# A two-block SwiGLU layer on one core: the first block's projections kept in written order, with row writes, loads and sums rearranged

## The chip, the cores and the metric

One core of one Trainium2 chip. The metric is the device time of one execution, in microseconds. Three runs of the kernel before gave 1728.53 (median), 1725.32 and 1729.53. The engines are named as the profile names them: PE is TensorE (PEld its weight loads), DVE is VectorE, ACT is ScalarE, POOL is GpSimd, SP is SyncE, which here only issues transfers.

## The reference, cut to what matters

One decoder layer on 1024 tokens of width 1024, in float32. The first and the last of its three sub-layers are SwiGLU feed-forward blocks (inner width 2816), between them stands a mix of sliding-window attention and a diagonal state-space model (SSM). Shift, scale and gate of each sub-layer come from one conditioning vector c:

```python
mod = silu(c) @ w_ada[l] + b_ada[l]
(sh1, sc1, ga1, sh2, sc2, ga2, sh3, sc3, ga3) = split(mod, 9)
h = rms_norm(x, g_pre_ff1) * (1 + sc1) + sh1
f = (silu(h @ w1_gate) * (h @ w1_up)) @ w1_down
x = x + 0.5 * ga1 * rms_norm(f, g_post_ff1)
...
```

The middle block adds `ga2 * rms_norm(mixed, g_post_mix)`, the last does as the first with sh3, sc3, ga3 and its own weights. The SSM's tables (powers of its eigenvalues, scaled input and output matrices) depend on parameters alone.

## The kernel before, in words

**Precision and products.** Every large operand is split into a high part rounded to fp32r, cast by ACT (L69), and a low part, the remainder, subtracted by DVE (L70). A product is three matmuls, high x high, high x low, low x high (`mm3`, L74 to L76). The gate and up projections and the down projection go by a Strassen-Winograd scheme: seven products of half-size blocks for eight, with sums and differences of blocks made on DVE.

**A feed-forward block.** `GateUp` computes column unit by column unit: an even unit is a gate, the next odd one the matching up projection. The first two units are computed plainly (`first`, then `first_done` with SiLU and product), since the sums of the activations (`s12`, `s34`) are not there yet. The other 20 units, u = 2 to 21, are in `rest`: for each, seven products in the order 1, 5, 6, 2, 7, 3, 4, each of 12 matmuls of 128x512, in all 140 products. `Weights.conv(i + 3)` (L287) first sees to it that the operands up to product i + 2 are converted: it forms a difference of weight blocks where the product wants one (L295 to L302), then the high and the low part, in one of four slots w0 to w3. `step` then issues the matmuls and what follows: product 1, 5 and 6 are copied out by ACT (L424 to L428), the next product of the chain adds to the same bank, DVE adds the others (L420), and then SiLU (even unit) or the product with the SiLU result (odd unit, L412). At the end of a pair of units four sums of result blocks (L383, `sums`) are written to DRAM for the down projection: on DVE in the first block, on POOL in the second. The results live in eight slots h0 to h7 in rotation, so the copy of product 1 of the next pair (c11) goes into a slot that the sums of the pair before still read.

**Beside the first block.** After each product a hook (`hook1`, L1353) runs. From product 4 on it keeps up to five rows of w_ada in flight (POOL issues the loads, 512 KB each) and reduces one of them on DVE against SiLU(c) to a column of `modc` (L141) at products with i % 8 in (0, 2, 3, 5, 6), 56 in all. After the last come `gate_row` and `scale_cols`: a gate column of 128x8 times its gain is written to DRAM as a row of 1024 (L152), to be read back later as a row broadcast to all partitions (`load_row`, L159). Then the twelve parts of the SSM preparation (`prep_steps`, L1036) follow, one at every third product: a long chain of operations on 128x16 tiles (`step_base`, with two exponentials `exp_`), angles and sines (`step_tw`), then products with transposes on PE (L1191) and small matmuls (L1226). They use slots q0 to q7.

**Then** the down projection (`down`, L453): six products over 11 steps each and a last one in pieces; the results of its first product are copied to q4 to q7 (L552). The mix follows, and the second block with no hook and no preparation.

**What sets the order.** The kernel is written for a framework that orders each engine's instructions when the program is built: an instruction is taken when it is ready by the scheduler's own estimate of time, and of those ready the one written earlier goes first. So an instruction whose inputs are there early can float far ahead of its place, and two products can be exchanged. `tc.keep_in_program_order(x)` ties x behind the instruction written just before it on the same engine; `tc.high_priority()` lets a section rank as if written earlier. The order is fixed on the chip.

## Time and profile before

| | |
|---|---|
| median of three runs | 1728.53 us (1725.32 to 1729.53) |
| profiled execution, its own time | 1731.16 us |
| its span, first to last instruction | 1729.2 us |
| mean granted PE clock | 0.982 |
| PE busy | 1661.3 us, 96% |
| DVE busy | 1261.4 us, 73% |
| ACT busy | 799.8 us, 46% |
| POOL busy | 201.5 us, 12% |
| chain that ended last, by engine | PE 81%, DVE 10%, ACT 3%, DMA 3%, issue 3% |

The page gives shares over the whole span, which mixes stages: PE is busy nearly always, so what matters is where it is not, and what ended each of these idle times. That is read from the windows (busy time by stage), the waits (who waited for whom) and the timeline (single instructions). A matmul's printed duration is longer than the time to the next one's start, since they are pipelined; losses are read from start to start.

### The profile page before, as it was taken

Reading aid. Unit: us, or ns where it says so; the run is one execution under the profiler, and the core shown is the slowest. Engines: PE = TensorE matmul, PEld = TensorE weight load, DVE = VectorE, ACT = ScalarE, POOL = GpSimd, SP = SyncE. Lnnn points to the kernel's source line nnn. Section 1 sums busy time; section 2 is a strip of 40 time slices with the busy share of each in tenths; the row PEclk is TensorE's granted clock in tenths of the full one; section 3 lists DMA queues with packets and bytes.
Section 4 is the critical chain, followed back from the end, with each engine's and each line's share of the span. In section 5 each row is a group of like instructions: output and inputs, shape, how many; then the busy total and the mean of one; then the engine's idle time right before and its main releaser. Section 6 shows DMA issues by size and latency. Waiting matters only on the chain.

```text
span 1729.2 us, 22074 instructions
## 1 busy us (share of the span) xinstructions
PE 1661.3 (96%) x7666; PEld 1357.8 (79%) x7666; DVE 1261.4 (73%) x2434; ACT 799.8 (46%) x1613; POOL 201.5 (12%) x198
## 2 busy tenths in 40 slices
PE   5999998999999999899989998999999999999998
PEld 4878777878787888688767886878888888888886
DVE  7988886899979658736479468776666555687586
ACT  4633333334334457746474157643333333354562
POOL 0011110110210000000003044011211111110001
PEclk8999999999999999899999999999999999999999
DMA  9156665633388342610053035222332323394334
GB/s 376 41 213 213 213 215 198 214 124 128 136 290 315 104 126 79 210 37 25 1 159 111 0 110 196 72 85 104 102 130 92 103 93 110 105 394 141 108 104 160
DMA packets 110624, 248.02 MB, mean 143 GB/s; under 512 B 11952, under 2 KB 27584, under 8 KB 110512
## 3 DMA queue, kind: packets, MB, share of 16 engines
q1 hardware_dynamic: 99776, 209.40, 35.5%
q0 software_dynamic: 10160, 36.16, 6.4%
q8 instruction: 60, 0.98, 0.2%
q10 hardware_dynamic: 576, 1.05, 0.2%
q14 instruction: 52, 0.43, 0.1%
HBM read 186.82 MB, written 59.75 MB: 143 GB/s over the span
## 4 chain that ended last, share of the span: by engine, by line
PE 81%; DVE 10%; ACT 3%; DMA 3%; issue 3%; POOL 0%; SPq 0%; DVEq 0%; ACTq 0%; POOLq 0%
PE b L76 25%; PE b L75 25%; PE b L74 25%; DVE a L70 2%; DVE w L70 1%; PE b L700 1%; PE b L788 1%; PE b L790 1%; PE b L789 1%; DMA g_d<-h 1%; PE b L734 1%; DMA t<-g_d 1%; ACT a L69 1%; PE b L172 0%; PE b L879 0%
## 5 line engine op out<-in xcount | busy, mean ns | idle before, releaser
L74 PE MATMUL b<-a,w 128*128 128x512 f32 x1260 | 493.9, 396 | 21.4 <-ACT w L69 10.0
L75 PE MATMUL b<-a,w 128*128 128x512 f32 x1260 | 495.8, 394 | 4.7 <-DVE a L70 4.7
L76 PE MATMUL b<-a,w 128*128 128x512 f32 x1260 | 488.0, 394 | 3.0 <-DVE w L70 3.0
L74 PEld LDWEIGHTS b<-a,w 128*128 128x128 f32 x1260 | 239.9, 191 | 77.3 <-ACT w L69 13.6
L75 PEld LDWEIGHTS b<-a,w 128*128 128x128 f32 x1260 | 239.8, 190 | 55.7 <-DVE a L70 6.2
L76 PEld LDWEIGHTS b<-a,w 128*128 128x128 f32 x1260 | 239.6, 190 | 56.0 <-DVE w L70 6.1
L69 ACT CAST w<-r 128x512 fp32r<-128x512 f32 (+1 forms) x210 | 130.8, 626 | 212.9 <-PE b L76 169.9
L70 DVE TENSOR_TENSOR w<-r,w 128x512 fp32r<-128x512 f32 (+1 forms) x206 | 151.5, 738 | 96.4 <-ACT w L69 96.4
L75 PE MATMUL b<-w,r 128*128 128x512 f32 x528 | 206.1, 391 | 2.1 <-DVE w L70 2.1
L76 PE MATMUL b<-w,r 128*128 128x512 f32 x528 | 205.7, 390 | 0.0
L74 PE MATMUL b<-w,r 128*128 128x512 f32 x528 | 177.6, 389 | 0.7 <-ACT w L69 0.7
L69 ACT CAST r<-a 128x512 fp32r<-128x512 f32 x110 | 68.5, 623 | 148.9 <-PE b L76 76.1
L70 DVE TENSOR_TENSOR r<-a,r 128x512 fp32r<-128x512 f32 x110 | 77.7, 706 | 76.3 <-ACT r L69 76.1
L420 DVE TENSOR_TENSOR h<-h,b 128x512 f32<-128x512 f32 x120 | 82.1, 685 | 56.7 <-PE b L76 50.9
L75 PEld LDWEIGHTS b<-w,r 128*128 128x128 f32 x528 | 99.7, 189 | 23.5 <-DVE w L70 2.8
L70 DVE TENSOR_TENSOR w<-t,w 128x512 fp32r<-128x512 f32 (+1 forms) x114 | 80.7, 709 | 49.1 <-ACT w L69 48.9
L74 PEld LDWEIGHTS b<-w,r 128*128 128x128 f32 x528 | 99.1, 188 | 21.7 <-ACT w L69 1.1
L76 PEld LDWEIGHTS b<-w,r 128*128 128x128 f32 x528 | 99.7, 189 | 20.6
L383 POOL TENSOR_TENSOR h<-h,h 128x512 f32<-128x512 f32 x44 | 72.1, 1650 | 367.4 <-DVE h L412 316.6
L69 ACT CAST w<-t 128x512 fp32r<-128x512 f32 (+1 forms) x114 | 70.3, 617 | 60.4 <-DVE t L298 27.6
L70 DVE TENSOR_TENSOR w<-a,w 128x512 fp32r<-128x512 f32 x110 | 77.4, 704 | 4.1 <-ACT w L69 3.9
L141 DVE CUSTOM_DVE_ANT_0 q<-q,c,cols 128x1024 f32<-128x1024 f32 x56 | 71.6, 1279 | 3.5 <-DMA q<-in_w_ada 3.5
(371 smaller groups left out, 2569.9 us busy)
## 6 DMA issues: line engine op xcount, KB each, us to landing
r<-in_w_gu SPq DMA_DIRECT2D x88, 512.0 KB, 4.1
g_d<-h SPq DMA_DIRECT2D x154, 256.0 KB, 3.1
q<-in_w_ada POOLq DMA_DIRECT2D x56, 512.0 KB, 4.7
a<-g_d SPq DMA_DIRECT2D x110, 256.0 KB, 2.8
a<-in_w_d SPq DMA_DIRECT2D x88, 256.0 KB, 5.4
a<-in_w_ada SPq DMA_DIRECT2D x16, 512.0 KB, 10.2
a<-in_x SPq DMA_DIRECT2D x12, 512.0 KB, 7.2
x_d<-a SPq DMA_DIRECT2D x12, 512.0 KB, 4.1
```

Source lines behind the costliest of these rows:

```text
L69: act.copy(hi, src)
L70: eng.tensor_tensor(lo, src, hi.bitcast(F32), op=SUB)
L74: pe.matmul(psum, wh, xh, start=first, stop=False, skip_group_check=goes_on)
L75: pe.matmul(psum, wh, xl, start=False, stop=False, skip_group_check=goes_on)
L76: pe.matmul(psum, wl, xh, start=False, stop=last, skip_group_check=goes_on)
L141: return dve.tensor_tensor_reduce(w, w, crow, 1.0, b_ada[:, j : j + 1], MUL, ADD, modc[:, j : j + 1])
L383: self.eng.tensor_tensor(d, x, y, op=op)
L420: dve.tensor_tensor(dst, dst, pb, op=ADD)
L700: pe.matmul(pb[kv][:, m % 2, ks], qT[m][rows, t * P : (t + 1) * P], kT[rows, (t + 1 - nk) * P : (t + 1) * P], start=True, stop=True,)
L734: pe.transpose(pt[:, m, :], pr[4 * kv + m][:, b * P : (b + 1) * P], ident)
L788: pe.matmul(pb, hh, wh, start=k == 0, stop=False)
L789: pe.matmul(pb, hh, wl, start=False, stop=False)
```

## The change

- A function `pinned` runs a function and ties each instruction that it writes behind the last one so written on the same engine. `rest` of the first block passes its `conv` and `step` through it, and `hook1` the column step (`ada_step`), so PE, ACT, DVE, POOL and SP take these in written order. The second block passes a plain call.
- `conv` is parted in two: `sum(n)` makes the loads and the difference for operand n, and is now called for the next operand behind the present one's low part.
- The columns are reduced at products with 1 <= i % 14 <= 8 (from product 4 on) instead of i % 8 in (0, 2, 3, 5, 6).
- A gate row is turned on PE (128x8 to 8x128) and copied by ACT to `rows`, and the write to DRAM takes eight rows of 128 numbers.
- The weights of unit 3 are loaded with those of unit 2, and the four sums of the first pair are written with high priority. These two and the parted `conv` hold for both blocks.
- In the preparation, the first operation of each exponential and the square of `are` are tied behind what is written before them on DVE.

```diff
@@ -74,6 +74,23 @@
...
         pe.matmul(psum, wl, xh, start=False, stop=last, skip_group_check=goes_on)
+
+    last_of = {}
+
+    def pinned(f, *args):
+
+        traced = nc.cur_bb.bb.instructions
+        n = len(traced)
+        r = f(*args)
+        for i in list(traced[n:]):
+            prev = last_of.get(i.engine)
+            if prev is not None:
+                tc.add_manual_dep(
+                    i, prev.name, mybir.DependencyInfo(mybir.DependencyClass.NoSync, mybir.DependencyReason.DATA),
+                    reason="pinned",
+                )
+            last_of[i.engine] = i
+        return r

...
@@ -90,6 +107,7 @@
...
     sink = cp.tile([P, NH], F32, name="sink")
+    rows = cp.tile([8, 3, P], F32, name="rows")

...
@@ -149,7 +167,10 @@
...
             dve.tensor_tensor(g, mod(v), gains[:, 2 * n + 1, :], op=MUL)
-        pool.dma_start(row_d[n].rearrange("(k p) -> p k", p=P), g)
+        pt = bank(tr_rot(), [P])
+        pe.transpose(pt[0:8, :], g, ident)
+        act.copy(rows[:, n, :], pt[0:8, :])
+        pool.dma_start(row_d[n].rearrange("(k p) -> k p", p=P), rows[:, n, :])

...
@@ -263,6 +284,7 @@
...
             self.raw, self.state, self.ops, self.n = {}, {}, {}, 0
+            self.src, self.summed = {}, set()
             self.r_rot = Rot(*names("r", 0, 1, 2, 3))
...
@@ -284,30 +306,39 @@
...

+        def sum(self, n):
+
+            if n >= len(self.seq) or n in self.summed:
+                return
+            self.summed.add(n)
+            u, m = self.seq[n]
+            for i in range(2):
+                self.load(u, i)
+            r0, r1, st = self.raw[u, 0], self.raw[u, 1], self.state[u]
+            b11, b12, b21, b22 = r0[:, 0], r0[:, 1], r1[:, 0], r1[:, 1]
+            if m == "5":
+                dve.tensor_tensor(b11, b12, b11, op=SUB)
+            if m == "6":
+                st["t2"] = slot(self.t_rot(), [512])
+                dve.tensor_tensor(st["t2"], b22, b11, op=SUB)
+            if m == "7":
+                dve.tensor_tensor(b12, b22, b12, op=SUB)
+            if m == "4":
+                dve.tensor_tensor(st["t2"], b21, st["t2"], op=SUB)
+            self.src[n] = {"1": b11, "6": st.get("t2"), "2": b21, "5": b11, "7": b12, "3": b22, "4": st.get("t2")}[m]
+
         def conv(self, upto):
...
                 u, m = self.seq[self.n]
-                for i in range(2):
-                    self.load(u, i)
-                r0, r1, st = self.raw[u, 0], self.raw[u, 1], self.state[u]
-                b11, b12, b21, b22 = r0[:, 0], r0[:, 1], r1[:, 0], r1[:, 1]
-                if m == "5":
-                    dve.tensor_tensor(b11, b12, b11, op=SUB)
-                if m == "6":
-                    st["t2"] = slot(self.t_rot(), [512])
-                    dve.tensor_tensor(st["t2"], b22, b11, op=SUB)
-                if m == "7":
-                    dve.tensor_tensor(b12, b22, b12, op=SUB)
-                if m == "4":
-                    dve.tensor_tensor(st["t2"], b21, st["t2"], op=SUB)
-                src = {"1": b11, "6": st.get("t2"), "2": b21, "5": b11, "7": b12, "3": b22, "4": st.get("t2")}[m]
+                self.sum(self.n)
                 op = slot(self.w_rot(), [2, 512], F32R)
-                split(op[:, 0], op[:, 1], src)
+                split(op[:, 0], op[:, 1], self.src.pop(self.n))
                 self.ops[u, m] = op
...
                         self.load(u + 2, i)
+                self.sum(self.n)

...
@@ -368,7 +399,8 @@
...
             if r == 1:
-                self.sums(0, [slot(o_rot(), [512]) for _ in range(4)])
+                with tc.high_priority():
+                    self.sums(0, [slot(o_rot(), [512]) for _ in range(4)])

...
@@ -383,7 +415,7 @@
...

-        def rest(self, hook):
+        def rest(self, hook, pin):
             U = {}
...
@@ -438,8 +470,8 @@
...
             for i, (u, m) in enumerate(wt.seq):
-                wt.conv(i + 3)
-                step(u, m)
+                pin(wt.conv, i + 3)
+                pin(step, u, m)
                 hook(i)
...
@@ -1045,7 +1077,7 @@
...
             y, n, r, q, m = T("ex_y"), T("ex_n"), T("ex_r"), T("ex_q"), T("ex_m")
-            dve.tensor_scalar(y, x, -150.0, 89.0, op0=MAX, op1=MIN)
+            tc.keep_in_program_order(dve.tensor_scalar(y, x, -150.0, 89.0, op0=MAX, op1=MIN))
             dve.tensor_scalar(n, y, 1.4426950408889634, BIG, op0=MUL, op1=ADD)
...
@@ -1134,7 +1166,7 @@
...
             dve.tensor_scalar(nr, pr[:, :, 1], 1.0, None, op0=SUB)
-            dve.tensor_tensor(t1, are, are, op=MUL)
+            tc.keep_in_program_order(dve.tensor_tensor(t1, are, are, op=MUL))
             dve.tensor_tensor(t2, aim, aim, op=MUL)
...
@@ -1337,6 +1369,8 @@
...
             g.wt.load(2, i)
+        for i in range(2):
+            g.wt.load(3, i)
         g.first_done(0)
...
@@ -1350,13 +1384,13 @@
...

-    def hook1(i):
+    def ada_step(i):
         if i >= 4 and (ada_rest or ada_raw):
...
                 ada_raw.append((j, ada_load(j, rest_rot())))
-            if i % 8 in (0, 2, 3, 5, 6):
-                tc.keep_in_program_order(ada_block(*ada_raw.pop(0)))
+            if 1 <= i % 14 <= 8:
+                ada_block(*ada_raw.pop(0))
             if not ada_raw:
...
@@ -1364,6 +1398,10 @@
...
                 prep.extend(prep_steps())
+
+    def hook1(i):
+        if ada_rest or ada_raw:
+            pinned(ada_step, i)
         elif prep and i % 3 == 0:
...
@@ -1373,7 +1411,7 @@
...

-    g1.rest(hook1)
+    g1.rest(hook1, pinned)
     ins, us, late, shares = mix_streams()
...
@@ -1427,7 +1465,7 @@
...
     second_half(g2)
-    g2.rest(lambda i: None)
+    g2.rest(lambda i: None, lambda f, *args: f(*args))
     down(2, a["w2_d"], None, lambda i: None, lambda: None)
...
```

## Rows read from the trace of the kernel before

**Rows 1.** Windows: the 140 products of each block (time, busy us and counts, clock, DMA)

```profile
84.80:495.20 410.40, 396.22 (x1762) 320.35 (x1761) 355.46 (x660) 151.22 (x264) 54.84 (x87) 0.99 0.54 182
1127.50:1512.60 385.10, 383.10 (x1682) 316.56 (x1681) 234.88 (x328) 142.72 (x245) 65.30 (x40) 1.00 0.31 103
```

**Rows 2.** Windows: the preparation's stage, the mix, and L1191's transposes alone (PE, PEld)

```profile
347.00:495.20 148.20, 146.27 (x687) 117.45 (x686) 140.51 (x273) 59.09 (x104) 22.76 (x28) 1.00 0.39 131
...
680.30:1127.50 447.20, 424.84 (x2176) 342.87 (x2174) 299.38 (x732) 254.79 (x632) 65.28 (x52) 0.96 0.29 94
...
84.80:495.20 410.40, 4.91 (x32) 3.83 (x32) 0.99 0.54 182
```

**Rows 3.** Waits of PE in the first block's 140 products, then in the second's

```profile
PE b L74 <- ACT h L424: 7.7, 2, 4.0
PE b L74 <- ACT w L69: 4.9, 8, 0.7
PE b L76 <- DVE w L70: 1.5, 2, 0.9
...
PE b L74 <- ACT h L424: 1.2, 1, 1.2
PE b L76 <- DVE w L70: 0.8, 1, 0.8
```

**Rows 4.** Timeline of PE at one short wait (start, us, instruction, idle before)

```profile
176.24 0.39 PE L76 MATMUL b<-a,w 128*128 128x512 f32 x1
177.34 0.50 PE L74 MATMUL b<-a,w 128*128 128x512 f32 x1 [0.71 <-ACT w L69]
```

**Rows 5.** Timelines of PE and ACT at the second long wait; window behind it

```profile
263.74 0.39 PE L76 MATMUL b<-a,w 128*128 128x512 f32 x1
268.11 0.72 PE L74 MATMUL b<-a,w 128*128 128x512 f32 x1 [3.98 <-ACT h L424]
268.63 0.63 PE L75 MATMUL b<-a,w 128*128 128x512 f32 x1
269.06 0.63 PE L76 MATMUL b<-a,w 128*128 128x512 f32 x1
...
267.47 0.59 ACT L424 COPY h<-b 128x512 f32<-128x512 f32 x1 [7.09 <-DMA g_d<-h]
...
268.30:271.30 3.00, 3.00 (x8) 2.32 (x9) 2.70 (x5) 1.91 (x4) 0.00 (x0) 0.50 0.26 98
```

**Rows 6.** DMA issues from 250.4 to 258.5 us (KB each, median us to landing)

```profile
g_d<-h SPq DMA_DIRECT2D x4, 256.0 KB, 11.9
row_d<-ggc POOLq DMA_DIRECT2D x1, 4.0 KB, 10.4
```

**Rows 7.** Timeline of PE at the first long wait

```profile
92.74 0.39 PE L76 MATMUL b<-a,w 128*128 128x512 f32 x1
96.88 0.50 PE L74 MATMUL b<-a,w 128*128 128x512 f32 x1 [3.75 <-ACT h L424]
```

**Rows 8.** Timelines of DVE and ACT ahead of that wait's end

```profile
88.49 0.68 DVE L368 TENSOR_TENSOR h<-h,b 128x512 f32<-128x512 f32 x1
89.09 3.09 DVE L70 TENSOR_TENSOR a<-q,a 128x512 fp32r<-128x512 f32 x5
...
92.86 0.68 DVE L383 TENSOR_TENSOR h<-h,h 128x512 f32<-128x512 f32 x1
...
96.24 0.59 ACT L424 COPY h<-b 128x512 f32<-128x512 f32 x1 [4.21 <-DVE h L383]
```

**Rows 9.** Groups of DVE instructions from 84.8 to 347 us (busy, mean ns, idle before)

```profile
L141 DVE CUSTOM_DVE_ANT_0 q<-q,c,cols 128x1024 f32<-128x1024 f32 x52 | 66.5, 1278 | 2.3 <-DMA q<-in_w_ada 2.3
...
L420 DVE TENSOR_TENSOR h<-h,b 128x512 f32<-128x512 f32 x37 | 25.3, 683 | 11.6 <-PE b L76 7.7 <-ACT h L426 3.6
...
L1055 DVE SCALAR_TENSOR_TENSOR ex_q<-ex_q,ex_r 128x16 f32<-128x16 f32 x6 | 1.0, 170 | 0.0
```

**Rows 10.** Timeline of PE in the down projection's second product

```profile
538.36 0.79 PE L75 MATMUL b<-w,r 128*128 128x512 f32 x1 [2.15 <-DVE w L70]
```

## The prediction

> **What bounds the kernel now.** TensorE's idle time by stage comes first. The rest of the first feed-forward block (20 column units times 7 products, 1680 matmuls) runs from 84.8 to 495.2 us, 410.4 us; the same 1680 matmuls of the second block, by the same code but with no adaLN columns and no SSM preparation beside them, from 1127.5 to 1512.6, 385.1 us [rows 1]. (The edges are the first matmul that reads a weight operand w against resident rows a, and the first of the down projection.) So TensorE bounds both, and the change can win at most about 25 us in its main place, less what the preparation's own transposes take there: 4.9 us for L1191 alone [rows 2], some 6 with L1226. Then the list of waits: in the first stretch TensorE waits 7.7 us in two pieces for the copy of c11 (L424), 4.9 us in eight pieces of up to 0.7 for a high part just cast (L69), and 1.5 us in two for a low part (L70), in all 14.1 us; in the second only one copy of 1.2 us and little else [rows 3]. The chain of waits says what must go for the two to be alike.
>
> **The eight short waits.** The pitch of the matmuls is 0.227 us (1680 of them in 385.1, its own small waits included, would give 0.229). A short wait costs more than the list says, because a matmul's printed end overlaps the next start: 176.24 to 177.34 is 1.10, a loss of 0.87 for a listed 0.71 [rows 4]. Eight waits of 0.61 on average plus 0.16 each: 6.2 us. They come where the scheduler swaps products at a unit's edge, so that an operand is cast only when its slot comes free. Written order converts operand i+2 before product i, and the operand's difference (0.68) is now issued behind the preceding low part, so the cast finds it done. DVE's load leaves room: by pair of units (14 products, 38 us) 8 differences, 14 low parts, 6 adds, 4 products and 4 result sums at the pitch of 0.60 (88.49 to 89.09 in [rows 8]) are 21.6 us, and 8 columns of 1.28 add 10.3: 32 of 38. I take **-6.2** (bounds -6.2 and 0), and for the two L70 waits, 1.5 plus 0.16 each, **-1.8** (bounds -1.8 and 0). Thinning spaces the 56 columns over products 4 to 101 instead of 5 to 93, and leaves none to the four-sum products at a pair's end. The column loads on POOL's queue keep five ahead; they and SP's loads and result writes now stand in written order too, with nobody near at hand behind them.
>
> **The row writes.** At 263.74 to 268.11 TensorE loses 4.14 us (start to start, less the pitch), then runs 8 matmuls at 0.43, at a granted clock of 0.50, the lower of the two levels, 1.2 GHz: 1.6 us more. The copy waited for a result write to land [rows 5]. One 4 KB row write took 10.4 us to land, and the results issued beside it 11.9 [rows 6]. Written as eight rows of 128 numbers it should cost no more than an ordinary transfer: **-5.7** (bounds -5.7, and 0 if the transfers queued for another reason). The other two row writes end no wait in the list.
>
> **The start.** TensorE stops from 92.74 to 96.88, a loss of 3.91 [rows 7], and then runs at the lower clock as after the other long wait, taken as 7 matmuls: 1.4 more. The c11 copy ran at 96.24, behind DVE's four result sums, issued from 92.86 on although their last input was there from 88.49 on [rows 8]. With priority the sums run from 89.09; the third ends near 91.0, the copy (0.59) at 91.6. Product 2, in written order, is due at 84.8 + 2 x 2.72 = 90.2, so 1.4 us remain, and about 0.4 for the low part that the sums push back. **-3.5** (bounds -5.3 and 0). The unit-3 loads, now ahead of two result writes on SP, only come sooner: nothing.
>
> **The gate rows.** New: after product 101 three transposes stand in TensorE's order, and they need DVE's add (pitch 0.60), the last column (about 1.28 [rows 9]) and the products behind it, some 0.2: 2.1 us. Then the transposes, and the third waits for ACT to empty the first bank; an 8x128 copy is in no row, the 128x512 copy takes 0.59 [rows 8]: 0.2 to 0.6. I take 2.8. An idle time of 2.15 was followed by half rate [rows 10], the waits of 0.71 were not [rows 4]: 8 x 0.2 = 1.6 more. **+4.4** (bounds +1.2 and +6).
>
> **The preparation.** It starts at product 102 instead of 96, and its scalar-sized chain, of which a part ran long before (six L1055 lie between 84.8 and 347 [rows 9]), follows too: some 4 to 5 us of DVE. From 347.0 to 495.2 DVE was busy 140.5 of 148.2 us [rows 2]. Six products less room is 16.3; minus 7.7 free plus 4.5 moved, some 13 us don't fit. I expect most of it to spill into the down projection, since in the kernel before DVE is just as full and TensorE hardly waits. **+1.5** (bounds 0 and the rival's price).
>
> **Second block.** Its sums are POOL's, idle until their input comes, so priority moves nothing; it has 2.0 us of waits to win [rows 3]. Zero (-2 to +2). All later stages are planned anew, since the order is computed for the whole program; TensorE idles 22.4 us from 680 to 1127.5 [rows 2], and a third of that either way, 6, goes into the range.
>
> **Sum.** -6.2 - 1.8 - 5.7 - 3.5 + 4.4 + 1.5 = -11.3 us. Against the profiled execution (1731.16, of which 1729.2 is span) that is 1719.9; that execution lies 2.63 above the median of the runs, 1728.53, so the forecast is **1717.2**. Check by the twin: 385.1, less its 2 us of waits and 1.4 of lower clock, plus 6 of preparation, 1.8 start, 4.4 rows and 1.5 is 395.3, against 410.4: -15. The sum is the more careful one.
>
> **Rivals.** *The gain is lost behind the stretch* (23%). Preparation that ends later holds the slots q4 to q7 into which the down projection's first four results are copied, and ACT's casts stand behind those copies; TensorE already waits 2.15 at 538 [rows 10]. For it: the 13 us above. Against: the banks are needed again only a whole product (30 us) later. Losing 8 of the 11.3 gives 1725.
>
> *The preparation starves the pinned products: slower* (14%). Its place is products 102 to 139; it decides if most of the 13 us of excess is paid by TensorE rather than spilled. DVE's adds wait there for TensorE, and low parts of later products now stand behind them and may not pass. Already in the freer order L420 stood idle 11.6 us, 7.7 of it for TensorE [rows 9]. Price: 13 us of excess, 7 more for low parts held behind adds (a third of a us in each of some 20 products), and about four waits over 2 us with 1.6 of lower clock each: 26. 1717.2 - 1.5 + 26 = 1742. Against: the preparation isn't pinned, and the order in the kernel before let the products' parts in between its operations. The Trainium skill ("TensorE: Matmul & The Clock Gate", section "Architectural detail: the array is 16x 32x32, not 1x 128x128") says that DVE's and ACT's queues are strictly first in, first out, so that nothing written later can slip past a waiting add; by that rule alone the pinned stretch would go this rival's way, by the idle row DVE stands as it says, but before, TensorE was not held up by it.
>
> *The order costs its own waits* (5%): TensorE, bound to written order, waits for the c11 copy at every pair, the change not doing what it says. Twenty waits of 0.5 give back 10 of 11.3: 1727. Against: the copy's sources are read 2.5 us after a pair ends, and the product that needs it comes 5.4 after.
>
> **How the numbers follow.** About 0.3% (5.2 us) can be told from no change: faster is under 1723.3, slower over 1733.7. The forecast has 58% (its own range 1707 to 1723: the bounds of rows and start, and half the replanning). With a little of the second case it makes faster 0.60; the rest of that and the fourth make same 0.25; slower 0.15. The range takes in the second and fourth: 1706 to 1734.
>
> **What would show it.** Right: the stretch from the first b<-a,w product to the first b<-w,r near 398 us; L69 gone from TensorE's list in it; no landing over 8 us about the second row write; one gap of 2 to 4 us before the gate rows' transposes; a start gap under 2. Wrong: L70 or DVE waits in the last 38 products, a stretch over 405, or a shorter stretch with new waits in the down projection or the mix.

## The result, and the profile after

The changed kernel takes 1734.59 us (median of six, 1731.57 to 1735.91), beside 1728.28 for the kernel before on the same chip (median of six): ratio 1.0035, 95% interval 1.0022 to 1.0048, slower by 4 to 8 us. The forecast was 1717.2, in a range of 1706 to 1734. The profiled execution of the changed kernel is the fastest of its six, 1731.57 with a span of 1729.8, and that of before is slower than its runs, 1731.16 with 1729.2. So the two traces are 0.6 apart where the medians are 6.3: they show where time came from and went to, but not the last 5 us.

Line numbers move by the diff: L383 is now L415, L412 L444, L420 L452, L424 L456, L552 L584, L1191 L1223, L1226 L1258. First the windows of the 140 products, the down projection and the second block's 140 products of the changed kernel (time, then busy us and counts of PE, PEld, DVE, ACT, POOL, then clock and DMA), which answer to [rows 1]; then the down projection of before.

```profile
83.40:474.30 390.90, 384.01 (x1696) 315.04 (x1695) 344.15 (x644) 145.21 (x260) 41.86 (x73) 1.00 0.54 185
474.30:685.20 210.90, 193.23 (x876) 157.11 (x876) 158.85 (x267) 100.37 (x182) 21.96 (x19) 0.94 0.50 174
1129.60:1512.40 382.80, 381.46 (x1681) 315.14 (x1680) 236.20 (x328) 143.00 (x245) 66.05 (x40) 1.00 0.31 104
```

```profile
495.20:680.10 184.90, 182.09 (x808) 149.58 (x807) 136.91 (x229) 97.79 (x174) 2.51 (x4) 0.99 0.54 186
```

The stretch became 19.5 us shorter (410.4 to 390.9) and began 1.4 earlier; the down projection behind it became 26.0 longer. The mix gave 3.0 and the second block's products 2.3; the end lost 0.8. Together +0.6, the difference of the spans. VectorE's column says the same from the other side: 11.3 us less in the stretch, 21.9 more in the down projection. Some 66 matmuls moved from one to the other, too (1762 to 1696, 808 to 876): the preparation's.

TensorE's waits in the changed kernel's stretch (total, times, longest), beside [rows 3]: all eight waits for L69 are gone, the long wait at 268 is gone, and the gate rows' wait (L171) is new.

```profile
PE b L74 <- ACT h L456: 3.0, 3, 2.5
PE b L171 <- DVE ggc L169: 2.2, 1, 2.2
PE b L76 <- DVE w L70: 1.5, 2, 1.1
```

Its timeline at the start, beside [rows 7], and at the gate rows; then the landing times of the three row writes (view of the tile row_d), beside the 10.4 of [rows 6]:

```profile
88.58 0.39 PE L76 MATMUL b<-a,w 128*128 128x512 f32 x1
91.46 0.50 PE L74 MATMUL b<-a,w 128*128 128x512 f32 x1 [2.49 <-ACT h L456]
...
363.37 0.39 PE L76 MATMUL b<-a,w 128*128 128x512 f32 x1
365.91 0.38 PE L171 MATMUL b<-ident,ggc 128*8 128x128 f32 x2 [2.15 <-DVE ggc L169]
366.53 0.38 PE L171 MATMUL b<-ident,ggc 128*8 128x128 f32 x1 [0.24 <-ACT rows L172]
366.56 0.77 PE L74 MATMUL b<-a,w 128*128 128x512 f32 x1
```

```profile
DMA to landing us min/median/max: 1.6/3.1/7.9
```

Now the down projection: TensorE's waits in the changed kernel, then in the kernel before.

```profile
PE b L1258 <- ACT c L1224: 9.1, 1, 9.1
PE b L75 <- DVE w L70: 2.6, 1, 2.6
PE b L1223 <- DVE q L1198: 2.0, 1, 2.0
PE b L1223 <- DVE q L1201: 2.0, 1, 2.0
PE b L1258 <- DVE q L1203: 1.9, 1, 1.9
```

```profile
PE b L75 <- DVE w L70: 2.1, 1, 2.1
PE b L74 <- ACT w L69: 0.7, 1, 0.7
```

17.6 us in five waits, four of them of the preparation's transposes (L1223) and small matmuls (L1258), which stand between the down projection's matmuls in TensorE's order. Here is their place in the timelines of TensorE, VectorE and ScalarE:

```profile
517.94 0.50 PE L75 MATMUL b<-w,r 128*128 128x512 f32 x1 [2.63 <-DVE w L70]
...
521.39 1.10 PE L1258 MATMUL b<-q,q 128*32 128x128 f32 x14 [1.92 <-DVE q L1203]
524.49 1.09 PE L1223 MATMUL b<-ident,q 128*128 128x128 f32 x4 [2.00 <-DVE q L1198]
527.57 1.09 PE L1223 MATMUL b<-ident,q 128*128 128x128 f32 x4 [1.99 <-DVE q L1201]
537.75 1.11 PE L1258 MATMUL b<-q,q 128*32 128x128 f32 x16 [9.09 <-ACT c L1224]
...
533.69 0.26 DVE L1267 SCALAR_TENSOR_TENSOR c<-delta,cols,c 128x16 f32<-128x16 f32 x1
...
528.69 0.59 ACT L584 COPY q<-b 128x512 f32<-128x512 f32 x1 [5.79 <-PE b L1223]
535.44 0.59 ACT L584 COPY q<-b 128x512 f32<-128x512 f32 x1 [6.17 <-DVE q L1201]
537.07 1.07 ACT L1224 COPY c<-b 128x512 f32<-128x512 f32 x2 [1.03 <-DMA kp_d<-c]
```

Four of the waits end with a VectorE operation. The longest, 9.1, ends with L1224, a copy of the preparation on ScalarE. It stands behind the copies of the down projection's first results into q4 to q7 (L584), and the second of these waited 6.17 us for the preparation's L1201, which by the code still read its slot, q5. (In the kernel before, these four copies start between 524.79 and 526.79, and none of them waits for VectorE.) The last 1.03 are for a write of the preparation that comes behind L1267, on VectorE at 533.69. So this wait, too, leads back to VectorE's preparation.

The window from the first of these waits on, whose clock (third from the end) is 0.50, the lower level:

```profile
520.00:544.00 24.00, 9.52 (x50) 6.88 (x51) 16.04 (x28) 3.85 (x8) 15.03 (x8) 0.50 0.44 157
```

The 26.0 us are 14.8 of waits (17.6 less 2.8), some 7.6 of the preparation's matmuls at the lower clock (8.2 busy, against 0.7 of them behind 495.2 before), and 3.6 left over, of which other matmuls at that clock are a part.

Why so late? L1203 closes each of the four wide products of the preparation; L1080 is the first operation of its chain of small ones (number of instructions, shortest, median and longest ns, first and last start). Before:

```profile
L1048 DVE TENSOR_SCALAR ex_y<-par x1: 166/166/166, 42.7 to 42.7; 128x16 f32<-128x16 f32 x1
...
L1171 DVE TENSOR_SCALAR q<-q x4: 447/452/461, 441.8 to 496.8; 128x576 f32<-128x576 f32 x4
```

After, and then the piece of VectorE's timeline where the chain begins:

```profile
L1080 DVE TENSOR_SCALAR ex_y<-par x1: 168/168/168, 371.7 to 371.7; 128x16 f32<-128x16 f32 x1
...
L1203 DVE TENSOR_SCALAR q<-q x4: 448/458/706, 467.4 to 535.4; 128x576 f32<-128x576 f32 x4
```

```profile
371.11 0.69 DVE L452 TENSOR_TENSOR h<-h,b 128x512 f32<-128x512 f32 x1 [2.67 <-PE b L76]
371.72 0.17 DVE L1080 TENSOR_SCALAR ex_y<-par 128x16 f32<-128x16 f32 x1
```

The chain once floated to 42.7; now it begins at 371.7, tied behind an add that itself waited 2.67 us for TensorE. The last of the wide products is closed 38.6 us later (535.4 against 496.8). What the ties have to do with that is tested below (e9, e10, e13).

### The profile page after: what moved, and what is told of

It reads as the page before. It is cut to its first block, busy times and chain, and to the rows that moved or that the text cites. A ratio compares the mean times of both kernels' runs of the same rounds, so it can differ in the third digit from the quotient of the medians.

```text
span 1729.8 us, 22152 instructions
## 1 busy us (share of the span) xinstructions
PE 1657.0 (96%) x7669; PEld 1357.3 (78%) x7669; DVE 1271.9 (74%) x2434; ACT 796.6 (46%) x1616; POOL 208.6 (12%) x198
## 4 chain that ended last, share of the span: by engine, by line
PE 49%; DVE 5%; ACT 2%; DMA 1%; issue 1%; POOL 0%; DVEq 0%; SPq 0%; ACTq 0%; POOLq 0%
PE b L75 14%; PE b L76 14%; PE b L74 14%; DVE a L70 1%; PE b L732 1%; PE b L820 1%; PE b L822 1%; PE b L821 1%; PE b L766 1%; ACT a L69 1%; PE b L911 0%; PE b L191 0%; DMA x_d<-q 0%; DMA r<-in_w_gu 0%; PE b L907 0%
## 5 line engine op out<-in xcount | busy, mean ns | idle before, releaser
L70 DVE TENSOR_TENSOR w<-r,w 128x512 fp32r<-128x512 f32 (+1 forms) x206 | 152.7, 742 | 92.2 <-ACT w L69 91.3
L69 ACT CAST w<-r 128x512 fp32r<-128x512 f32 (+1 forms) x210 | 130.6, 625 | 157.7 <-PE b L76 92.8
L69 ACT CAST r<-a 128x512 fp32r<-128x512 f32 x110 | 68.5, 623 | 147.1 <-PE b L76 84.7
L70 DVE TENSOR_TENSOR r<-a,r 128x512 fp32r<-128x512 f32 x110 | 77.8, 707 | 74.9 <-ACT r L69 74.8
L452 DVE TENSOR_TENSOR h<-h,b 128x512 f32<-128x512 f32 x120 | 82.4, 687 | 57.6 <-PE b L76 56.6
L415 POOL TENSOR_TENSOR h<-h,h 128x512 f32<-128x512 f32 x44 | 72.8, 1666 | 365.4 <-DVE h L444 314.3
L70 DVE TENSOR_TENSOR w<-t,w 128x512 fp32r<-128x512 f32 (+1 forms) x114 | 80.9, 710 | 41.6 <-ACT w L69 41.5
L69 ACT CAST w<-t 128x512 fp32r<-128x512 f32 (+1 forms) x114 | 70.1, 615 | 68.8 <-PE b L76 20.6
L70 DVE TENSOR_TENSOR w<-a,w 128x512 fp32r<-128x512 f32 x110 | 77.4, 704 | 0.9 <-ACT w L69 0.8
L74 PE MATMUL b<-a,a 128*128 128x512 f32 x182 | 71.2, 394 | 1.1 <-DVE r L939 1.1
```

Of the source, the lines that this page charges most:

```text
L69: act.copy(hi, src)
L70: eng.tensor_tensor(lo, src, hi.bitcast(F32), op=SUB)
L74: pe.matmul(psum, wh, xh, start=first, stop=False, skip_group_check=goes_on)
L415: self.eng.tensor_tensor(d, x, y, op=op)
L452: dve.tensor_tensor(dst, dst, pb, op=ADD)
```

## The experiments

Theories when they began. **A:** the preparation's small products stand in TensorE's queue inside the down projection, and the order alone makes the waits. **B:** VectorE's work is the bound: its 67 us of preparation begin too late, and what doesn't fit before the down projection is paid there, wherever TensorE's order puts it. **C:** the one GpSimd copy of L1249 that took 10.5 us holds up the rest. Each ratio is against the kernel before on the same chip, by medians.

**e1, columns ended earlier.**

```diff
-            if 1 <= i % 14 <= 8:
+            if i % 14 not in (5, 6, 12, 13):
```

> Edit: columns at ten of fourteen products instead of eight, so that the preparation starts near product 82 instead of 102. In the profile of the changed kernel TensorE waits 17.6 us between 517.9 and 538.8 us, four times for the preparation's small products (L1223, L1258), and runs at the lower clock for 23.9 us there. Theory A (the preparation's last products stand in TensorE's order inside the down projection and hold it): in this kernel's order all of them stand before the down projection, so about 26 us go: 1709 (1704 to 1715). Theory B (VectorE is simply too full around the start of the down projection, whoever waits): its work is only moved forward, 34.5 of 38 us in each pair of units are then taken, and part of the wait moves with it: 1720 to 1730. Theory C (one slow GpSimd copy of 10.5 us did it): it depends on whether it meets VectorE's stream again, 1712 to 1730.

1727.76, ratio 0.9966 [0.9945, 0.9987]. No wait in the down projection (182.0 us); the stretch has 408.0, with 12.3 of waits, 3.3 of them at the gate rows. With the preparation in time the down projection loses nothing. The stretch is 17 us longer than the changed kernel's: TensorE is busy 11.2 longer in it, since the preparation's matmuls come back, and waits 5.4 more. That a denser VectorE makes these waits is not shown: e8, below, has more of VectorE's work there (366.1 us against 363.4) and a shorter stretch.

**e2, the copies of L1249 on ScalarE.**

```diff
-                    pool.tensor_copy(bd[64 * gp : 64 * gp + 64, :, :, gp, :], ...)
+                    act.copy(bd[64 * gp : 64 * gp + 64, :, :, gp, :], ...)
```

> Edit: the preparation's eight 64x128 copies into the block-diagonal tile run on ScalarE instead of GpSimd, where one took 10.5 us. Theory A: the other waits for the preparation stay (8.5 us and the lower clock), only the last of 9.1 goes or shrinks: 1721 to 1727. Theory B: no change, 1733 to 1736. Theory C (the slow copy, with the write queued behind it on GpSimd, is the main price): the 9.1 us wait and half of the lower-clock loss go: 1716 to 1721.

1732.76, ratio 1.0002 [0.9980, 1.0025]. The wait shrinks by 1 us and the others stay: C falls. (The ratio is 0.0033 below the changed kernel's, with intervals that just overlap; in the traces the two are 1.1 us apart.)

```profile
PE b L1258 <- ACT c L1224: 8.1, 1, 8.1
```

**e3, without the preparation's transposes and small matmuls on TensorE** (ScalarE copies other data of the same shape).

```diff
-                        pe.transpose(pt[:, k, :], g[:, k].rearrange("p j h -> p (j h)"), ident)
...
-                        pe.matmul(
-                            pk[32 * g : 32 * g + 32, :],
...
```

> Edit: the preparation's transposes and small matmuls on TensorE are left out, ScalarE copies other data of the same size in their place, so the state-space tables are not computed; VectorE's and GpSimd's work stays. TensorE's own time for them, some 7 us, goes in any case: 1728 by that alone. Theory A: the waits in the down projection go as well, since nothing of the preparation stands in TensorE's order: 1702 to 1708. Theory B: VectorE is as full as before and the products' low parts are as late: 1724 to 1729. Theory C: nobody waits for the slow copy any more but the write behind it: 1704 to 1712.

1724.81, ratio 0.9945 [0.9922, 0.9969]. With nothing of the preparation in TensorE's order the down projection still waits 11.8 us, now for its own operands and its emptied banks (the last 0.6 is for L69):

```profile
PE b L74 <- ACT q L584: 5.8, 2, 2.9
PE b L75 <- DVE w L70: 5.4, 3, 2.4
```

A alone falls: order decides which instruction waits. The 5.8 us for L584 are banks that the copies into q4 to q7 emptied late. (The 8 us of those matmuls are saved as well, so the total tells less than the list.)

**e4, columns spread as before, the rest changed.**

```diff
-            if 1 <= i % 14 <= 8:
+            if i % 8 in (0, 2, 3, 5, 6):
```

> Edit: the columns back at i % 8 in (0, 2, 3, 5, 6), nothing else, so the preparation starts at product 96. Its last small product then stands 110 matmuls into the down projection in TensorE's order, against 156. Theory A: the waits shrink but stay, 1722 to 1730. Theory B: 16 us earlier start of the same work: 1728 to 1733. If thinning the columns is what keeps the pinned stretch free of waits, new short waits of 0.35 us appear at pair boundaries, 2 us in all.

1724.06, ratio 0.9946 [0.9913, 0.9978]. Stretch 400.5; down projection 185.8 with 0.3 of waits. Neither theory had that: A let the waits shrink and stay, B left the time as it was. In the stretch no wait for L69 comes back, but these do, four of them 0.83 long:

```profile
PE b L76 <- DVE w L70: 4.3, 7, 0.8
```

**e5, the angle steps keep one of their ten VectorE operations** (18 us left out).

```diff
-            dve.tensor_tensor(t, V["fl"][:, gs].unsqueeze(2).broadcast_to(sh), cv, op=MUL)
-            for i in range(2):
-                dve.tensor_scalar(n, ang, BIG, None, op0=ADD)
...
-            dve.scalar_tensor_tensor(n, ang, -1.0, ang, op0=MUL, op1=MIN)
```

> Edit: in the changed kernel the preparation's angle steps keep one of their ten VectorE operations per quarter, so some 18 of its 67 us of VectorE work are left out and the rotation tables are not computed; its transposes and small matmuls on TensorE stay where the scheduler puts them. Without TensorE's share of the preparation (e3) 11.8 us of waits for low parts stayed in the down projection. Theory A (order on TensorE is the cause): the waits in the down projection shrink only as far as the last small products move forward; a third stays, 8 to 12 us below the kernel before at best 6. Theory B (VectorE's amount of work between product 102 and the end of the second down product is the cause, and TensorE's order only says where it is paid): with 18 us less the 17.6 us of waits and the lower clock behind them go: 18 to 24 us below the changed kernel, 12 to 18 below the kernel before.

1721.52, ratio 0.9963 [0.9950, 0.9976]. The down projection waits 0.5 us and takes 183.0: 18 us less of VectorE's work remove 17 us of TensorE's waits. But part comes back in the stretch (405.0, with 10.7 of waits), because the preparation's products now come into it, so that the total is some 6 us below the kernel before where B had 12 to 18.

**e6, without the program order of the 140 products.**

```diff
-    g1.rest(hook1, pinned)
+    g1.rest(hook1, lambda f, *args: f(*args))
...
-            pinned(ada_step, i)
+            ada_step(i)
```

(and the columns tied as in the kernel before)

> Edit: the changed kernel without the tying of the first block's products and columns to written order; all else of the change stays, the preparation's own two ties too. If the order is what took the eight short waits away, they come back (6 us in the 140 products), the start and the row write stay repaired; the stretch is then 396 to 404 us against 391. Theory B: VectorE's work in the down projection's start is the same less what moved, so waits there shrink by what the stretch loses, and the total stays within 5 us of the changed kernel. Theory A: the preparation's small products stand equally late (156 matmuls into the down projection), so the whole 26 us stay and the total is 5 to 10 us above the changed kernel.

1739.45, ratio 1.0061 [1.0046, 1.0076]. The stretch is the shortest of all, 389.1, and the down projection the longest, 216.3 with 23.3 of waits, one of them 15.4. Its waits for L69 in the stretch (beside them stands one of 0.3 for L70):

```profile
PE b L74 <- ACT w L69: 3.4, 9, 1.0
```

The first is 1.0; the other eight, one at the end of a pair, are 0.30 each, where the kernel before has waits of up to 0.74. So without the order the short waits are shorter, but not gone. Between A and B the total settles nothing: 4.5 us above the changed kernel by the ratios, where B allowed up to 5 and A began there. The stretch was expected at 396 to 404, a miss.

**e7, the kernel before with the turned row writes alone.**

```diff
-        pool.dma_start(row_d[n].rearrange("(k p) -> p k", p=P), g)
+        pt = bank(tr_rot(), [P])
+        pe.transpose(pt[0:8, :], g, ident)
+        act.copy(rows[:, n, :], pt[0:8, :])
+        pool.dma_start(row_d[n].rearrange("(k p) -> k p", p=P), rows[:, n, :])
```

> Edit: the kernel before with the row writes alone changed (turned on TensorE, copied by ScalarE, written as eight rows). By the step of the forecast: the wait of 4.0 us for a result write behind the second row write and 1.6 us of lower clock go, and the turned rows cost less than 4.4 us since nothing ties them: 1 to 6 us below the kernel before. If transfers queue there for another reason than the row write's shape: no gain, 0 to 4 us above.

1725.96, ratio 0.9983 [0.9973, 0.9993]. The stretch is 6.1 us shorter (404.3), the wait at 268 is gone, the eight short ones stay (5.1 us); later stages give back some of it.

**e8, columns in one more place of each 14, rows turned a product later each.**

```diff
-            if 1 <= i % 14 <= 8:
+            if 1 <= i % 14 <= 9:
...
-                gate_row(0, 2, True)
+                late_rows.append(gate_row(0, 2, True))
...
-        elif prep and i % 3 == 0:
-            prep.pop(0)()
+        else:
+            if late_rows:
+                pinned(late_rows.pop(0))
+            if prep and i % 3 == 0:
+                prep.pop(0)()
```

> Edit: the changed kernel with columns at nine of fourteen products (none at a pair's end), the preparation from product 90 on, and the three turned rows each a product later than the gate columns, so that TensorE does not stand before VectorE's column. Theory B: the preparation gets 12 products, 33 us, more room and its 67 us fit before the second down product; the down projection's waits of 17.6 us and 12 us of lower clock go, and so does the stop of 2.2 us with its 1.6 of lower clock before the rows; new waits of 2 to 5 us in the stretch: 24 to 30 us below the changed kernel, 15 to 22 below the kernel before. Theory A: much the same, since no small product stands in the down projection any more. If neither holds (something else in the down projection is slow): within 8 us of the changed kernel.

1714.16, ratio 0.9919 [0.9904, 0.9933]: below both kernels, 14 us below the one before, where B had 15 to 22. The windows of its stretch and its down projection, and the closing operation of its wide products:

```profile
83.20:483.00 399.80, 393.09 (x1768) 319.35 (x1767) 366.10 (x684) 149.83 (x271) 52.18 (x91) 0.99 0.56 190
483.00:665.00 182.00, 182.00 (x804) 150.70 (x803) 136.35 (x227) 96.17 (x170) 0.65 (x1) 1.00 0.53 181
```

```profile
L1207 DVE TENSOR_SCALAR q<-q x4: 446/449/454, 428.4 to 471.8; 128x576 f32<-128x576 f32 x4
```

VectorE does 22 us more in the stretch than in the changed kernel and 22.5 less behind it, and TensorE has no wait in the down projection. The stretch is 8.9 longer, the down projection 28.9 shorter.

**e9, the kernel before with the thinned columns alone.** (e8's column line, with 8 instead of 9.)

> The kernel before with the thinned columns alone (nothing in 9 to 13 of each 14 products, steps otherwise and orders as before). Theory B (VectorE's amount of work between the preparation's start and the end of the second half's down projection is the bound; thinning starts the preparation six products later and takes about 20 us of waits out of TensorE's time): the short waits behind L69 and L70 in the 140 products vanish, some 6 to 8 us, but the preparation's tail stands 156 products into the down projection and waits of 10 us or more come up there; the total is 3 to 11 us above the kernel before. If instead the lost time after the change comes from the tied order or the new row writes and not from thinning: no wait over 1 us in the down projection and 3 to 6 us below the kernel before.

1727.84, ratio 0.9987 [0.9968, 1.0006]: between the two forecasts, and for the total a miss of both. The parts are those of B: the short waits nearly vanish, the down projection loses what the stretch wins (400.0 and 195.2, against 410.4 and 184.9), with 8.7 of waits. TensorE's waits in the stretch, and the last wide product:

```profile
PE b L74 <- ACT h L424: 7.0, 2, 3.7
PE b L74 <- ACT w L69: 0.9, 3, 0.3
```

```profile
L1171 DVE TENSOR_SCALAR q<-q x4: 449/454/460, 462.9 to 528.4; 128x576 f32<-128x576 f32 x4
```

So thinning by itself takes most of the short waits away, and it wins nothing. The chain of the preparation is not tied here and starts at 42.8, and still the last wide product is closed 31.6 us later than in the kernel before. Some 5.0 us of that may be one wait of VectorE for a load of the preparation (L1246, up to 377.54), which stands in the lists of neither the kernel before nor the changed one.

**e10, the changed kernel without the preparation's two ties.**

```diff
-            tc.keep_in_program_order(dve.tensor_scalar(y, x, -150.0, 89.0, op0=MAX, op1=MIN))
+            dve.tensor_scalar(y, x, -150.0, 89.0, op0=MAX, op1=MIN)
...
-            tc.keep_in_program_order(dve.tensor_tensor(t1, are, are, op=MUL))
+            dve.tensor_tensor(t1, are, are, op=MUL)
```

> The changed kernel without the program order of the preparation (its steps may be moved by the scheduler; the first projections stay in program order). Theory B: a few us of VectorE's work go ahead into idle places of the stretch, its tail stands 138 instead of 156 products into the down projection, and the waits there shrink from 17.6 us to 8 to 14: 4 to 10 us below the changed kernel. If VectorE's amount is not the point (the rival: order on TensorE's queue alone), the preparation's small products wait as long as before and the time stays within 2 us of the changed kernel.

1721.28, ratio 0.9946 [0.9922, 0.9971]: 13 us below the changed kernel by medians (15 by the ratios), more than B allowed. One wait of 3.6 is left in the down projection. VectorE's waits from 355 to 480 us, the changed kernel's and then e10's, and e10's preparation:

```profile
DVE w L70 <- ACT w L69: 4.0, 6, 1.4
DVE h L452 <- PE b L76: 3.1, 3, 2.7
DVE r L70 <- ACT r L69: 1.7, 2, 1.3
```

```profile
DVE w L70 <- ACT w L69: 0.7, 2, 0.5
DVE r L70 <- ACT r L69: 0.3, 1, 0.3
DVE h L452 <- PE b L76: 0.2, 1, 0.2
```

```profile
L1080 DVE TENSOR_SCALAR ex_y<-par x1: 172/172/172, 360.1 to 360.1; 128x16 f32<-128x16 f32 x1
...
L1203 DVE TENSOR_SCALAR q<-q x4: 445/452/771, 451.1 to 506.3; 128x576 f32<-128x576 f32 x4
```

In these lists 8.8 us of waits against 1.2. The chain begins 11.6 us earlier, fills places in which VectorE otherwise stood, and the wide products end 29 us earlier. Two lines of the diff, which look like nothing, make the difference here between a loss and a gain; which of the two it is was not tried.

**e11 and e12, two variants of e8:** columns in 1 to 10; and e8 without the program order of the products.

> The version with columns in positions 1 to 9 of each 14 products (1714.2 us), with columns in 1 to 10, so that the preparation starts about ten products earlier still. Theory B: VectorE has then room to spare, the down projection stays free of waits as it is with nine, and nothing more is won there; fewer free products at the end of each pair bring back waits of a few tenths to 2 us in the 140 products: within 4 us of the version with nine, rather above. If an earlier preparation still pays: 2 to 4 us below it.

> The version with columns in positions 1 to 9 (1714.2 us), without the program order of the 140 products. Theory B: the products run ahead as in the changed kernel without that order (389 us for the stretch), the preparation's tail then stands 100 products into the down projection, and VectorE's backlog is paid there: 5 to 20 us above the version with nine. If the order is worth nothing once the preparation starts in time: within 2 us of it.

e11: 1717.34, ratio 0.9929 [0.9900, 0.9958], the same as e8 within the intervals; down projection 182.0 without waits, stretch 401.2. e12: 1721.56, ratio 0.9945 [0.9924, 0.9965], some 4.5 above e8 by the ratios, with intervals that overlap, and less than the 5 to 20 expected; stretch 394.6, down projection 186.9. The products' order is worth about that here, as it is between e6 and the changed kernel (1.0061 and 1.0035).

**e13, e14, e15.** e13 is the changed kernel with both e4's and e10's edits, e14 is e8 with e10's edit, e15 the changed kernel with e8's column line alone.

> The changed kernel with both taken back: columns again at i % 8 in (0, 2, 3, 5, 6), and the preparation's two ties gone. One cause that needs both (VectorE full by the thinning, and kept by the ties from working ahead in its waits): with either gone the waits in the down projection are gone already, so the second one adds little: 1718 to 1724, within 4 us of e4 and e10. Two causes that add up: 10 us for the thinning and 13 for the ties below the changed kernel, some 1711 or less.

> The version with columns in positions 1 to 9 and the turned rows a product later (e8, 1714.2), without the preparation's two ties. If the ties cost only where VectorE has no time to spare: within 3 us of e8, since e8 has no wait in the down projection. If they cost by themselves: 5 us or more below e8, by shorter waits in products 90 to 139.

> The changed kernel with columns in positions 1 to 9 of each 14 products as its only edit; the gate rows are turned where the change turns them. By the theory of VectorE's amount of work the earlier start of the preparation is what e8 lives on: no wait over 1 us in the down projection, the gap of some 2 us at the turned rows is back with its lower clock, so 2 to 5 us above e8, 1716 to 1720. If instead the rows' place matters for the preparation too: waits in the down projection, 1722 or more.

e13: 1719.19, ratio 0.9929 [0.9894, 0.9963]. By the ratios (times 1728.3) the square is: thinned and tied +6.0 us; either one undone -9.3; both undone -12.3. Two costs adding up would give -24.6, a ratio of 0.986, outside e13's interval. The delays do add up, though: the last wide product is closed at 482 with neither, at 506 with the thinning alone, at 508 with the ties alone, and at 535 with both. What the down projection waits for them does not: 0.5, 3.6, 0.3 and 17.6 us. In the changed kernel it bears each delay alone nearly for nothing, and both together not. e14: 1712.41, ratio 0.9881 [0.9828, 0.9933], not to be told from e8: where the preparation is in time, the ties cost nothing that shows. e15: 1724.31, ratio 0.9963 [0.9937, 0.9989], a miss: the down projection has no wait, as expected, but the gate rows' gap is 2.7 and 5.0 us of further waits follow it up to 408 (stretch 403.8), and mix and second block take 6 more than in e8. The rows' place is worth more than the 2 to 5 us I gave it; how much of the 6 behind is its doing is open, and the late rows with eight columns were not tried.

All versions that do the whole of the work (us; from the profiled executions; "columns" and "wide" are the starts of the last column of L159 and of the last operation of the wide products):

| | columns | wide | stretch | down | PE waits in down | ratio |
|---|---|---|---|---|---|---|
| e1 | 313 | 467 | 408.0 | 182.0 | 0 | 0.9966 |
| e11 | 304 | 459 | 401.2 | 182.0 | 0 | 0.9929 |
| e14 | 333 | 469 | 397.0 | 182.6 | 0.3 | 0.9881 |
| e15 | 334 | 469 | 403.8 | 182.0 | 0 | 0.9963 |
| e8 | 334 | 472 | 399.9 | 182.0 | 0 | 0.9919 |
| e13 | 348 | 482 | 402.6 | 183.0 | 0.5 | 0.9929 |
| e7 | 351 | 491 | 404.3 | 187.1 | 3.2 | 0.9983 |
| before | 357 | 497 | 410.4 | 184.9 | 2.8 | 1 |
| e12 | 342 | 503 | 394.6 | 186.9 | 1.3 | 0.9945 |
| e10 | 365 | 506 | 398.1 | 190.6 | 3.6 | 0.9946 |
| e4 | 348 | 508 | 400.5 | 185.8 | 0.3 | 0.9946 |
| e9 | 369 | 528 | 400.0 | 195.2 | 8.7 | 0.9987 |
| after | 364 | 535 | 390.9 | 210.9 | 17.6 | 1.0035 |
| e2 | 365 | 536 | 391.1 | 208.8 | 16.6 | 1.0002 |
| e6 | 367 | 540 | 389.1 | 216.3 | 23.3 | 1.0061 |

While the wide products end by 508 the down projection waits at most 3.6 us; at 528 it is 8.7, at 535 17.6 and at 540 23.3, with the lower clock on top. The three shortest stretches are those whose preparation ends last.

## Why the prediction was wrong

**Short waits, -6.2 and -1.8: right in size.** The eight of L69 and the two of L70 are gone (two other L70 waits, 1.5 together, stand in the preparation's place and belong to it). The reason I gave, written order, is only a part of it. In the kernel before, thinning by itself leaves 0.9 of the 6.4 us (e9). In the changed kernel it takes both: thinned without the order, nine waits for L69 of 3.4 us in all are left (e6); in order without thinning none for L69, but seven for L70 of 4.3 (e4).

**Row writes, -5.7: right.** The writes land in 1.6 to 7.9 us, no result waits for them, and alone they shorten the stretch by 6.1 (e7), of which the total keeps 2.9.

**Start, -3.5: nearly.** The gap is 2.49 where 1.8 was forecast, with a loss of 2.65 (91.46 less 88.58, less the pitch) in place of 3.91, and the clock stays up this time, so -2.7. That it stayed up is luck: behind the same gap of 2.49, e8 has 3.4 us at a clock of 0.51 (92.00 to 95.40).

**Gate rows, +4.4: right.** 363.37 to 366.56 is 2.96 over the pitch, and up to 369.99 the lower clock behind it adds 1.6: 4.6. But I costed it on TensorE alone. The add of L452 waits for TensorE there, and the preparation's chain stood behind that add.

**The preparation, +1.5: this is the step that failed.** In the stretch it cost only about 2.7 (four waits of 2.0 us in all, plus 0.16 each). The count was low: some 13 us of VectorE's work that would not fit, where 21.9 moved. And what was wrong is the sentence "I expect most of it to spill into the down projection, since in the kernel before DVE is just as full and TensorE hardly waits". It spilled, and there it cost 26.0. The kernel before bore its preparation until 497; I took that for room, and it was near the edge, as the table shows. I moved its end by 20.8 us at most (six products, 16.3, and 4.5 of small operations); it moved by 38.6. Two delays make that up. Thinning is worth 24 to 32 us in the three pairs that show it (e13 and e10, e4 and the changed kernel, the kernel before and e9). The two ties, which I priced as work and not as a delay, are worth 26 to 29 (e13 and e4, e10 and the changed kernel). The rest of the change takes some 15 back (the kernel before and e13). That the chain starts 329 us later says little: e9's starts at 42.8 and its wide products end at 528, e13's at 337.1 and they end at 482. The chain's end says more. Its last operation (L1158, now L1190) starts 6.5 us behind the last column in the kernel before (363.1), 18 and 23 behind it without the ties (e10, e13), and 35 and 37 with them (the changed kernel, 399.6, and e4). With the ties gone, e10 ends the chain 16 us earlier and the wide products 29 us earlier, and is 13 us faster.

**The rivals.** "The gain is lost behind the stretch" named the place and part of the mechanism, but priced it at 8, on the ground that the banks are needed again only a product later. Its copies into q4 to q7 did wait for the preparation (6.17 us at 535.44), but what TensorE stood for first was what came behind them in ScalarE's queue, a copy of the preparation (9.1 us); the other preparation waits were for VectorE directly. With the preparation's products away, late operands and, for 5.8 us, the banks themselves are what TensorE waits for (e3). "The preparation starves the pinned products" had the mechanism, adds that wait for TensorE with others behind them that may not pass, and a price of 26; it put both into the wrong stage. I held against it that the preparation isn't pinned. Its first steps were. The Trainium skill ("TensorE: Matmul & The Clock Gate", section "Architectural detail: the array is 16x 32x32, not 1x 128x128") says that DVE's queue is strictly first in, first out; the rows at 371.11 and 371.72 agree, and e10, where the chain was put ahead of that add when the order was made, shows what it cost. "The order costs its own waits" did not come: beside the start's, the c11 copy is waited for twice, 0.5 us together.

**Stretch, forecast near 398, measured 390.9.** Some of this was never a gain: TensorE left 56 of the preparation's matmuls behind (24 transposes and 32 small ones, some 6 us at the pace they have in the kernel before), and VectorE 22 us of work. What I listed as a sign of being wrong, "a shorter stretch with new waits in the down projection", is what came. The check by the twin (its terms add up to 395.4) should have warned me: it can say how short the stretch gets, not who pays for work pushed out of it.

**Later stages, 0:** the mix and the second block together gave 5.3 in the traces compared, within the 6 of the range. What separates 0.6 (traces) from 6.3 (medians) stays open.

## What to carry to other kernels

Before waits are taken out of the bounding engine, count what the other engines did in that time: work that ran beside it needs a new place, and what the next stage can bear is read from how late that work ended before, not from a short list of waits. A tie on a tiny operation at the head of a long chain is priced by what ends the chain and by what it now stands behind in its queue. And two delays that the next stage bears one at a time it may not bear together. Here an earlier start of the side work (nine columns of 14 products for eight, the turned rows a product later) turned 0.35% above the kernel before into 0.8% below it (e8), 1.2% without the ties (e14, an interval that overlaps).

## What the runs showed of the hardware

- **One GpSimd copy took 10.5 us.** L1249 in the changed kernel (view of one line: shortest, median and longest ns):

```profile
L1249 POOL COPY q<-q x8: 284/720/10508, 404.9 to 533.3; 64x128 f32<-64x128 f32 x8
```

Eight copies of one shape, with a median of 0.72. The long one ran from 522.69; VectorE, with operations of two inputs each, was busy 10.47 of the 10.51 us, and its only gap, at 533.04, came just before the copy ended. The Trainium skill ("SBUF — State Buffer", section "🔬 SBUF: two separate sides") says that a VectorE operation with two SBUF inputs and a GpSimd one that reads SBUF exclude each other at a shared pair of ports: whichever starts first holds the pair for the whole instruction, and the other blocks fully. The trace fits a copy that found no gap; that it waited for the ports is not shown. It was not the cause of the wait all the same (e2: 8.1 instead of 9.1), and VectorE was as late.

- **A stretch at the lower clock can be much longer than others of its kind.** In the profiled execution of e4 the clock is 0.50 for 30.7 us in the mix; at the same place the other versions show 6.8 or 10.2. e4's runs lie between 1718.18 and 1733.69. The window:

```profile
895.00:925.70 30.70, 28.82 (x87) 21.68 (x88) 23.09 (x37) 11.34 (x23) 9.41 (x10) 0.50 0.25 68
```

- **Stages that no edit touches move.** The mix took 443.1 to 455.3 us and the second block's products 382.7 to 387.4 over these versions. The order of the whole program is made anew each time, which may be why; a gain of 5 us in one stage can be lost or doubled by that.
